# The last token group's gate stage by column halves, with the six last weight blocks run tile by tile

## The chip, the cores and the metric

The kernel runs on one core of a Trainium2 chip. A core has five engines that run side by side: TensorE (PE, matmuls), VectorE (DVE), ScalarE (ACT), GpSimd (POOL) and SyncE (SP, which here only issues DMAs). Each executes its own instructions strictly in the order in which the program lists them, and semaphores make one wait for another. The metric is device time in microseconds; the kernel before took 2855.22 us (median of three runs, 2851.17 to 2855.67).

## What is computed

One bidirectional encoder layer with shared weights runs over two sequences, a prompt of 512 tokens and a sample of 1024. The change touches the last step alone, the per-layer embedding, for the last 512 tokens of the sample:

```python
gate = jax.nn.sigmoid((group_rmsnorm(h, ple_norm_pre) @ w_ple_gate).astype(f32))
e = (p_l @ w_ple_proj).astype(f32)
h = h + group_rmsnorm((gate * e).astype(dtype), ple_norm_post)
```

`group_rmsnorm` divides a row of 1024 numbers by the root of its mean square and multiplies by a weight row. So for each token: gate times e, the sum of its squares over all 1024 columns, a scale from that sum, times the weight row, plus the residual h, and out.

## The kernel before

Tokens are worked in groups of 512, four tiles of 128 tokens each (`ORDER` is 0, 2, 1, 3). The sample has two groups, S 0 and S 1; S 1 is the last work of the program.

`ple` (L1374) makes the gate with `tok_gemm` (L1007), a matrix product of the group's 512 tokens with `w_ple_gate` (1024 by 1024). It does the 1024 output columns in two halves `nch` of 512. Within a half it goes over the 1024 input rows in blocks of 128, loaded in pairs (`k0` = 0, 2, 4, 6). Since products in fp32 are made of a rounded and a low part, a block is loaded (SP, L277, into `wst`), rounded on ACT (L292, `whi`), and its low part is made on POOL (L293, `wlo`). Each block and tile then takes three matmuls of 512 columns (`mm3`, L301 to L303). `whi` and `wlo` have six buffers each, so six blocks fit. Normally all four tiles take a pair of blocks before the next pair. In the second half of the last products (`last`) two pairs are held back and run tile by tile, so that tiles end one after another:

```python
                if last and nch == 1 and k0 + 4 >= nk:
                    if k0 + 2 < nk:
                        continue
                for t in ORDER:
                    for u0, ws in units:
```

After a half, `ev_gate` (L1383) applies the sigmoid on ACT (L1386, `mst`) and multiplies the tile's half of e by it on VectorE (L1387; the tile `ga`, which lives in the buffers named `bh`).

`ple_post` (L1392) calls `post_steps` (L1040), written for whole rows of 1024: residual load `load` (L1050, SP), `sumsq` (L312, an ACT square with accumulator, which is a second ACT instruction), `rstd` (L305: a 128x1 scalar operation on VectorE, L308, and a power on POOL, L309), then `add`. For S 1 (`last`), `add` makes the product with the weight row (L1056) ahead of the scale, then scale and residual in one instruction (L1057), and stores 128x1024 from SP (L1061). `post` runs at high priority.

The order of instructions on each engine is not the order of the code: the framework schedules them by a simulated timeline and by priorities.

Of the kernel before, what the change touches and what calls it, by code (L numbers as in the profile page):

```python
# [15 lines left out]
ALU = mybir.AluOpType  # L16
PSUM = bass.MemoryType.PSUM

D = 1024
# [3 lines left out]
NF = FFN // 128  # L23
# [143 lines left out]
class Kern:  # L167
# [143 lines left out]

    def sumsq(self, pool, x):  # L312

        ss = self.T(self.sp, [128, 1], "ss")
        junk = self.T(pool, [128, x.shape[-1]], "junk", BF16, bufs=1)
        self.nc.scalar.activation(junk, x, AF.Square, accum_out=ss)
        return ss
# [689 lines left out]
    def tok_gemm(self, lhs, nk, wsrc, krow0, evac, last=False, mid=None):  # L1007

        for nch in range(2):
# [7 lines left out]
            for k0 in range(0, nk, 2):  # L1017
# [3 lines left out]
                if mid and nch == 0 and k0 == 4:  # L1021
                    mid()
                if last and nch == 1 and k0 + 4 >= nk:
                    if k0 + 2 < nk:
                        continue
# [13 lines left out]

    def post_steps(self, pool, acc, row, res, t0, dst, gain=None, u=None, tags=("t4",) * 4, last=False):  # L1040


        nc = self.nc
# [4 lines left out]
        def load(t):  # L1048
            rts[t] = self.T(pool, [128, 1024], tags[t])
            nc.sync.dma_start(rts[t], res[t0 + t * 128:t0 + (t + 1) * 128, :])  # L1050

        def add(t):
            a, r, rt = acc[t], rs[t], rts[t]
            if last:
                w = self.T(pool, [128, 1024], "t4")
                nc.vector.tensor_tensor(out=w, in0=a, in1=rw, op=ALU.mult)  # L1056
                nc.vector.scalar_tensor_tensor(rt, w, r, rt, ALU.mult, ALU.add)  # L1057
            else:
                nc.vector.scalar_tensor_tensor(a, a, r, rw, ALU.mult, ALU.mult)
                nc.vector.tensor_tensor(out=rt, in0=a, in1=rt, op=ALU.add)  # L1060
            (nc.sync if last else nc.gpsimd).dma_start(dst[t0 + t * 128:t0 + (t + 1) * 128, :], rt)  # L1061
            if gain:
                rs[t] = self.rstd(self.sumsq(pool, rt), D)
# [36 lines left out]
    def outproj(self, q, g, pool, acc, k0, mix, u=None):  # L1100
# [10 lines left out]
        last = k0 + nk == 16  # L1111
        self.tok_gemm(mix.tok, nk, self.I["w_out"][0], k0 * 128, evac, last)
        if last:
# [8 lines left out]
    def down(self, pool, acc, hidden, m0, cnt):  # L1122

        nc = self.nc

        def evac(nch, t, ps):
            a = acc[t][:, nch * 512:(nch + 1) * 512]
            if m0 == 0:
                nc.scalar.activation(a, ps, AF.Copy)
            else:  # L1130
                nc.vector.tensor_tensor(out=a, in0=a, in1=ps, op=ALU.add)

        self.tok_gemm(lambda k, t: [x[:, t * 128:(t + 1) * 128] for x in hidden[m0 + k]], cnt,
                      self.I["w_down"][0], m0 * 128, evac, m0 + cnt == NF)

# [238 lines left out]
    def ple(self, q, g, pool, u):  # L1374
# [3 lines left out]
        def load():  # L1378
            for t in ORDER:
                r0 = g * 512 + t * 128  # L1380
                nc.sync.dma_start(ga[t], q.e[r0:r0 + 128, :])

        def ev_gate(nch, t, ps):  # L1383
            a = ga[t][:, nch * 512:(nch + 1) * 512]
            sg = self.T(pool, [128, 512], "mst")
            nc.scalar.activation(sg, ps, AF.Sigmoid)  # L1386
            nc.vector.tensor_tensor(out=a, in0=a, in1=sg, op=ALU.mult)  # L1387

        self.tok_gemm(u.tok, 8, I["w_ple_gate"][0], 0, ev_gate, True, load)
        return ga  # L1390

    def ple_post(self, q, g, pool, ga):  # L1392
        last = q is self.S and g == 1
        self.post(pool, ga, "ple_norm_post", q.h2, g * 512, q.out, last=last,
                  tags=("bh", "bl", "bl", "bh") if last else ("t4",) * 4)

    def build(self):
# [43 lines left out]
        with self.pool("mix_s", side="right") as mp, ExitStack() as right:  # L1441
# [24 lines left out]
            with self.pool("blocks") as tb:  # L1466
# [21 lines left out]
                with self.pool("end_s", side="right") as tr:  # L1488
# [5 lines left out]
                    self.rush(chain)  # L1494
                    for g, v in ((0, v0), (1, v1)):
                        self.ple_post(S, g, pe, self.ple(S, g, pe, v))

# [29 lines left out]
```

## Time and profile before

| | us |
|---|---|
| median of three runs | 2855.22 |
| lowest and highest run | 2851.17, 2855.67 |
| the profiled execution | 2852.23 |
| its span, first to last instruction | 2850.3 |
| PE busy in the span | 2683.8 (94%) |
| DVE busy | 1742.6 (61%) |
| POOL busy | 1380.7 (48%) |
| ACT busy | 1336.4 (47%) |
| mean granted TensorE clock | 0.98 |

Times in the profile are microseconds from the start of the span. A timeline row gives start, length, engine, line, operation and tiles (written <- read), the number of instructions merged into it, and in brackets how long the engine was idle before it and what ended that. A group row gives the count, busy time, mean in nanoseconds, and idle time. PEld is the weight load of a matmul, which overlaps the one before. A window row gives the busy time and the number of instructions of each engine in a stretch, then the granted clock, the busy share of the 16 DMA engines, and their GB/s. "SPq" and "ACTq" are instructions of an engine's queue that are not counted as busy, such as the issue of a DMA.

### The profile page before, as it was taken

What the parts mean: (1) busy time and instruction counts of PE and PEld (TensorE: products, weight loads), DVE (VectorE), ACT (ScalarE), POOL (GpSimd) and SP (SyncE); (2) the same over time, 40 slices, a digit from 0 to 9 for tenths busy, and PEclk for the clock granted to TensorE, in tenths of its full rate; (3) what the DMA queues carried; (4) which work ended last, traced back from release to release, by engine and by line L of the source; (5) the groups of instructions that cost most, each with busy time, mean ns of one, the idle gap of its engine ahead of it and who ended that gap; (6) DMA issues with size and microseconds to landing.
All of it is one profiled execution on the core that took longest, in us unless ns stands there. A gap on an engine that the chain in (4) does not pass through costs nothing.

```text
span 2850.3 us, 41685 instructions
## 1 busy us (share of the span) xinstructions
PE 2683.8 (94%) x14696; PEld 2254.9 (79%) x14696; DVE 1742.6 (61%) x2893; ACT 1336.4 (47%) x2580; POOL 1380.7 (48%) x1137
## 2 busy tenths in 40 slices
PE   7999999999999989889999998987799999999998
PEld 5987888778888767578778776766699999877776
DVE  6767896977666896966676734475343444325345
ACT  4434445773234564745444454365533333344453
POOL 4445555443453556535444444554454444445464
PEclk9999999999999999989999999999999999999999
DMA  5544555744345576778888886565632222366665
GB/s 169 180 137 127 150 174 185 219 141 138 99 123 160 154 249 202 223 206 206 199 181 204 187 218 218 177 222 183 157 100 82 79 75 86 119 207 207 203 202 186
DMA packets 448507, 480.04 MB, mean 168 GB/s; under 512 B 29409, under 2 KB 330281, under 8 KB 445995
## 3 DMA queue, kind: packets, MB, share of 16 engines
q1 hardware_dynamic: 340923, 347.34, 40.0%
q0 software_dynamic: 28224, 68.17, 10.8%
q10 hardware_dynamic: 79152, 61.88, 6.9%
q8 instruction: 116, 1.90, 0.3%
q14 instruction: 92, 0.75, 0.1%
HBM read 346.54 MB, written 91.95 MB: 154 GB/s over the span
## 4 chain that ended last, share of the span: by engine, by line
PE 66%; DVE 15%; DMA 8%; issue 5%; POOL 3%; ACT 2%; SPq 0%; POOLq 0%; ACTq 0%; DVEq 0%
PE g L301 17%; PE g L303 16%; PE g L302 16%; PE a L302 3%; PE a L303 3%; PE a L301 3%; PE a L700 1%; DVE b L692 1%; DVE W L619 1%; DVE E L615 1%; PE a L973 1%; POOL wlo L293 1%; DMA wlo<-wst 1%; PE a L404 1%; DMA mx<-mix_s 1%
## 5 line engine op out<-in xcount | busy, mean ns | idle before, releaser
L293 POOL TENSOR_TENSOR wlo<-wst,whi 128x512 fp32r<-128x512 f32 (+1 forms) x544 | 786.1, 1452 | 756.6 <-ACT whi L292 691.5
L292 ACT ACTIVATE whi<-wst 128x512 fp32r<-128x512 f32 (+1 forms) x544 | 339.5, 628 | 532.9 <-PE g L302 330.0
L301 PE MATMUL g<-uh,whi 128*128 128x512 f32 (+1 forms) x1232 | 493.5, 401 | 8.5 <-DVE cv L393 4.4
L303 PE MATMUL g<-uh,wlo 128*128 128x512 f32 (+1 forms) x1232 | 491.6, 399 | 0.0
L302 PE MATMUL g<-ul,whi 128*128 128x512 f32 (+1 forms) x1232 | 490.9, 398 | 0.0
L301 PE MATMUL g<-bh,whi 128*128 128x256 f32 x1056 | 293.0, 283 | 14.3 <-ACT sc L1266 3.8
L303 PE MATMUL g<-bh,wlo 128*128 128x256 f32 x1056 | 294.0, 281 | 4.2 <-DMA wlo<-mx 2.7
L302 PE MATMUL g<-bl,whi 128*128 128x256 f32 x1056 | 294.3, 280 | 0.0
L301 PEld LDWEIGHTS g<-uh,whi 128*128 128x128 f32 x1232 | 233.2, 189 | 67.5 <-issue 10.4
L303 PEld LDWEIGHTS g<-uh,wlo 128*128 128x128 f32 x1232 | 232.6, 189 | 53.9 <-issue 5.8
L302 PEld LDWEIGHTS g<-ul,whi 128*128 128x128 f32 x1232 | 232.9, 189 | 53.4 <-issue 7.2
L326 DVE TENSOR_TENSOR ml<-mx,mh 128x512 fp32r<-128x512 f32 x152 | 122.4, 808 | 222.0 <-ACT mh L325 221.9
L285 POOL DMA_DIRECT2D wlo<-wst x144 | 126.0, 930 | 226.2 <-ACT wlo L284 211.1
L393 DVE SCALAR_TENSOR_TENSOR cv<-g,cols,cv 128x510 f32<-128x510 f32 (+3 forms) x192 | 193.0, 1006 | 64.9 <-ACT cv L387 62.8
L301 PEld LDWEIGHTS g<-bh,whi 128*128 128x128 f32 x1056 | 197.2, 189 | 20.0 <-DVE gt L1227 6.1
L303 PEld LDWEIGHTS g<-bh,wlo 128*128 128x128 f32 x1056 | 199.6, 189 | 4.9 <-DMA wlo<-mx 2.9
L302 PEld LDWEIGHTS g<-bl,whi 128*128 128x128 f32 x1056 | 199.5, 189 | 0.1
L301 PE MATMUL g<-whi,mh 128*128 128x512 f32 x412 | 169.7, 412 | 23.7 <-ACT mh L325 16.3
L302 PE MATMUL g<-wlo,uh 128*128 128x264 f32 (+1 forms) x576 | 191.3, 332 | 0.5 <-POOL wlo L293 0.5
L303 PE MATMUL g<-whi,ul 128*128 128x264 f32 (+1 forms) x576 | 189.9, 331 | 1.6 <-DVE rs_t L308 1.6
L309 POOL TENSOR_TENSOR rs_t<-rs_t,nhalf 128x1 f32<-128x1 f32 (+2 forms) x112 | 120.0, 1074 | 144.0 <-DVE rs_t L308 141.5
L301 PE MATMUL g<-whi,uh 128*128 128x264 f32 (+1 forms) x576 | 189.0, 330 | 0.0
(334 smaller groups left out, 6030.5 us busy)
## 6 DMA issues: line engine op xcount, KB each, us to landing
wst<-in_w_in SPq DMA_DIRECT2D x192, 256.0 KB
wlo<-wst POOLq DMA_DIRECT2D x144, 256.0 KB, 4.9
wst<-in_w_down SPq DMA_DIRECT2D x132, 256.0 KB
wst<-in_w_out SPq DMA_DIRECT2D x96, 256.0 KB
wst<-in_w_gate SPq DMA_DIRECT2D x92, 256.0 KB
wst<-in_w_up SPq DMA_DIRECT2D x92, 256.0 KB
mx<-hid_s SPq DMA_DIRECT2D x88, 256.0 KB
rw<-rows_s SPq DMA_DIRECT2D x32, 512.0 KB
```

What stands on the lines that cost most here:

```text
L285: nc.gpsimd.dma_start(lo, w, accum_op=ALU.add)
L292: nc.scalar.activation(hi, w, AF.Copy)
L293: (eng or nc.gpsimd).tensor_tensor(out=lo, in0=w, in1=hi.bitcast(F32), op=ALU.subtract)
L301: nc.tensor.matmul(ps, lh, rh, start=first, stop=False, skip_group_check=shared)
L302: nc.tensor.matmul(ps, lh, rl, start=False, stop=False, skip_group_check=shared)
L303: nc.tensor.matmul(ps, ll, rh, start=False, stop=last, skip_group_check=shared)
L309: nc.gpsimd.tensor_tensor(out=t[:, :w], in0=t[:, :w], in1=self.nhalf[:, :w], op=ALU.pow)
L326: self.nc.vector.tensor_tensor(out=lo, in0=ps, in1=hi.bitcast(F32), op=ALU.subtract)
L393: nc.vector.scalar_tensor_tensor(out[:, a:b], ps[:, a + d:b + d], wcol(w), out[:, a:b], ALU.mult, ALU.add)
L404: nc.tensor.transpose(ps[:, j * 128:(j + 1) * 128], srcs[i + j], self.ident)
L615: nc.vector.scalar_tensor_tensor(E[:, h], rw[:, 0, h], dbf[:, c, gh:gh + 1], rw[:, 1, h], ALU.add, ALU.min)
L619: nc.vector.scalar_tensor_tensor(W[:, h], su, dt[:, c, gh:gh + 1], W[:, h], ALU.mult, ALU.add)
```

## The change

For S 1 (`end`), `ple` now does everything, and `ple_post` isn't called:

- the square is done for each half of the columns, into `hs`, and the two sums are added on VectorE when the second half is there (L1396 of the changed kernel);
- the product with the weight row is done for each half, in place (L1390);
- the residual is loaded inside the first half's evaluation (L1393), into two `t4` buffers (tiles 0 and 1) and two `bl` buffers (tiles 2 and 3), before two `bh` and two `bl`;
- scale and residual are done as two halves (L1400), each stored by itself (L1401), the first from SP and the second from ACT;
- in the second column half three pairs of blocks are held back in place of two (`last` = 3), so blocks 2 to 7 run tile by tile;
- nothing of it runs at high priority any more.

`last` of other products becomes 2, which leaves them as they were; `post_steps` loses its `last` branch.

```diff
-                if last and nch == 1 and k0 + 4 >= nk:
+                if last and nch == 1 and k0 + last * 2 >= nk:
...
+        end = q is self.S and g == 1
+        hs = self.T(self.sp, [128, 2, 4], "hss", bufs=1) if end else None
+        res = {}
+
         def ev_gate(nch, t, ps):
             a = ga[t][:, nch * 512:(nch + 1) * 512]
             sg = self.T(pool, [128, 512], "mst")
             nc.scalar.activation(sg, ps, AF.Sigmoid)
             nc.vector.tensor_tensor(out=a, in0=a, in1=sg, op=ALU.mult)
-
-        self.tok_gemm(u.tok, 8, I["w_ple_gate"][0], 0, ev_gate, True, load)
+            if not end:
+                return
+            self.sumsq(pool, a, hs[:, nch, t:t + 1])
+            nc.vector.tensor_tensor(out=a, in0=a, in1=rw[:, nch * 512:(nch + 1) * 512], op=ALU.mult)
+            if nch == 0:
+                res[t] = self.T(pool, [128, 1024], "t4" if t < 2 else "bl")
+                nc.sync.dma_start(res[t], q.h2[g * 512 + t * 128:g * 512 + (t + 1) * 128, :])
+                return
+            ss = hs[:, 0, t:t + 1]
+            nc.vector.tensor_tensor(out=ss, in0=ss, in1=hs[:, 1, t:t + 1], op=ALU.add)
+            r = self.rstd(ss, D)
+            for i, eng in enumerate((nc.sync, nc.scalar)):
+                cs = slice(i * 512, (i + 1) * 512)
+                nc.vector.scalar_tensor_tensor(res[t][:, cs], ga[t][:, cs], r, res[t][:, cs], ALU.mult, ALU.add)
+                eng.dma_start(q.out[g * 512 + t * 128:g * 512 + (t + 1) * 128, cs], res[t][:, cs])
+
+        if end:
+            rw = self.gain_row(pool, "row", "ple_norm_post")
+        self.tok_gemm(u.tok, 8, I["w_ple_gate"][0], 0, ev_gate, 3 if end else 2, load)
...
-                    for g, v in ((0, v0), (1, v1)):
-                        self.ple_post(S, g, pe, self.ple(S, g, pe, v))
+                    self.ple_post(S, 0, pe, self.ple(S, 0, pe, v0))
+                    self.ple(S, 1, pe, v1)
```

What this makes of the order on three engines is shown at three places. First PE, in the second column half of S 1, from the 7th matmul behind blocks 0 and 1. Before, where `a_27149` and `a_27151` are the accumulators of tiles 0 and 2, and `whi_27191` and `whi_27197` blocks 2 and 3:

```order
L301 MATMUL a_27151<-whi_27191,bh_26472 128x512
L302 MATMUL a_27151<-wlo_27192,bh_26472 128x512
L303 MATMUL a_27151<-whi_27191,bl_26476 128x512
L301 MATMUL a_27151<-whi_27197,bh_26472 128x512
L302 MATMUL a_27151<-wlo_27198,bh_26472 128x512
```

In the changed kernel, where `a_27172` and `a_27174` are tiles 0 and 2, and `whi_27214`, `27220`, `27226`, `27232` blocks 2 to 5 (27238 and 27244, further on, are blocks 6 and 7):

```order
L301 MATMUL a_27172<-whi_27226,bh_26473 128x512
L302 MATMUL a_27172<-wlo_27227,bh_26473 128x512
L303 MATMUL a_27172<-whi_27226,bl_26477 128x512
L301 MATMUL a_27172<-whi_27232,bh_26473 128x512
L301 MATMUL a_27174<-whi_27214,bh_26472 128x512
L302 MATMUL a_27174<-wlo_27215,bh_26472 128x512
L302 MATMUL a_27172<-wlo_27233,bh_26473 128x512
L303 MATMUL a_27172<-whi_27232,bl_26477 128x512
L303 MATMUL a_27174<-whi_27214,bl_26476 128x512
```

Tile 0 goes on with blocks 4 and 5 where tile 2 had blocks 2 and 3, and the scheduler has put tile 2's matmuls between tile 0's; the two share the first 36 of the 72 matmuls, and tiles 1 and 3 follow with 18 each. The low part of block 6 is used first by the 27th of the 72, that of block 7 by the 32nd.

Second ACT, at the end of the first column half of S 1 (g_26987 and g_26990 hold tiles 0 and 2, g_26988 and g_26991 tiles 1 and 3; the four `whi` are blocks 4 to 7 of the second half). Before:

```order
L1386 ACTIVATE mst_27137<-g_26987 128x512
L1386 ACTIVATE mst_27140<-g_26987 128x512
L292 ACTIVATE whi_27227<-wst_27225 128x512
L1386 ACTIVATE mst_27143<-g_26988 128x512
L1386 ACTIVATE mst_27146<-g_26988 128x512
L292 ACTIVATE whi_27233<-wst_27231 128x512
L292 ACTIVATE whi_27239<-wst_27237 128x512
L292 ACTIVATE whi_27245<-wst_27243 128x512
```

In the changed kernel:

```order
L1385 ACTIVATE mst_27140<-g_26990 128x512
L1385 ACTIVATE mst_27148<-g_26990 128x512
L316 ACTIVATE junk_27143,hss_26987<-bh_26983 128x512
L292 ACTIVATE whi_27226<-wst_27224 128x512
L316 ACTIVATE junk_27151,hss_26987<-bh_26985 128x512
L1385 ACTIVATE mst_27156<-g_26991 128x512
L1385 ACTIVATE mst_27164<-g_26991 128x512
L292 ACTIVATE whi_27232<-wst_27230 128x512
L316 ACTIVATE junk_27159,hss_26987<-bh_26984 128x512
L316 ACTIVATE junk_27167,hss_26987<-bh_26986 128x512
L292 ACTIVATE whi_27238<-wst_27236 128x512
L292 ACTIVATE whi_27244<-wst_27242 128x512
```

Four squares stand among the roundings of the last four blocks.

Third VectorE, at the end of the program (bh_26984 is tile 1, bh_26986 tile 3 in both). Before:

```order
L1387 TENSOR_TENSOR bh_26986<-bh_26986,mst_27306 128x512
L1057 SCALAR_TENSOR_TENSOR bl_27347<-t_5322_27349,rs_t_27330,bl_27347 128x1024
L1056 TENSOR_TENSOR t_5324_27355<-bh_26986,row_27309 128x1024
L308 TENSOR_SCALAR rs_t_27336<-ss_27333 128x1
L1057 SCALAR_TENSOR_TENSOR bh_27353<-t_5324_27355,rs_t_27336,bh_27353 128x1024
```

In the changed kernel (t_5278_27162 and bl_27170 are the residuals of tiles 1 and 3; the rows marked x2 are two halves):

```order
L1386 TENSOR_TENSOR bh_26984<-bh_26984,mst_27348 128x512
L1390 TENSOR_TENSOR bh_26984<-bh_26984,row_26988 128x512
L1396 TENSOR_TENSOR hss_26987<-hss_26987 128x1
L1386 TENSOR_TENSOR bh_26986<-bh_26986,mst_27362 128x512
L308 TENSOR_SCALAR rs_t_27355<-hss_26987 128x1
L1400 SCALAR_TENSOR_TENSOR t_5278_27162<-bh_26984,rs_t_27355,t_5278_27162 128x512 x2
L1390 TENSOR_TENSOR bh_26986<-bh_26986,row_26988 128x512
L1396 TENSOR_TENSOR hss_26987<-hss_26987 128x1
L308 TENSOR_SCALAR rs_t_27369<-hss_26987 128x1
L1400 SCALAR_TENSOR_TENSOR bl_27170<-bh_26986,rs_t_27369,bl_27170 128x512 x2
```

Behind the last gate product (L1387 before, L1386 now), tile 1's two final halves still stand ahead of tile 3's row product, as tile 1's final product did before. On ACT, the two stores of tiles 0 and 2 stand ahead of tile 1's square.

On POOL nothing changes its place. On SP, the first two residual loads (now tiles 2 and 3) stand a few places later, behind the first loads of e for S 1; that of tile 0 stands between the weight loads of blocks 4 and 5 of the second half, that of tile 1 behind block 7.

More of the change, by code (lines that the diff above doesn't have):

```diff
@@ L310, in rstd, with sumsq @@
         return t[:, :w]
-    def sumsq(self, pool, x):
-        ss = self.T(self.sp, [128, 1], "ss")
+    def sumsq(self, pool, x, ss=None):
+        ss = self.T(self.sp, [128, 1], "ss") if ss is None else ss
         junk = self.T(pool, [128, x.shape[-1]], "junk", BF16, bufs=1)
@@ L1038, in post, with post_steps @@
             pass
-    def post_steps(self, pool, acc, row, res, t0, dst, gain=None, u=None, tags=("t4",) * 4, last=False):
+    def post_steps(self, pool, acc, row, res, t0, dst, gain=None, u=None):
         nc = self.nc
@@ L1048, in load @@
         def load(t):
-            rts[t] = self.T(pool, [128, 1024], tags[t])
+            rts[t] = self.T(pool, [128, 1024], "t4")
             nc.sync.dma_start(rts[t], res[t0 + t * 128:t0 + (t + 1) * 128, :])
@@ L1053, in add @@
             a, r, rt = acc[t], rs[t], rts[t]
[L1054 to L1061, printed above, removed]
+            nc.vector.scalar_tensor_tensor(a, a, r, rw, ALU.mult, ALU.mult)
+            nc.vector.tensor_tensor(out=rt, in0=a, in1=rt, op=ALU.add)
+            nc.gpsimd.dma_start(dst[t0 + t * 128:t0 + (t + 1) * 128, :], rt)
             if gain:
@@ L1111, in outproj @@
         last = k0 + nk == 16
-        self.tok_gemm(mix.tok, nk, self.I["w_out"][0], k0 * 128, evac, last)
+        self.tok_gemm(mix.tok, nk, self.I["w_out"][0], k0 * 128, evac, 2 * last)
         if last:
@@ L1133, in down @@
         self.tok_gemm(lambda k, t: [x[:, t * 128:(t + 1) * 128] for x in hidden[m0 + k]], cnt,
-                      self.I["w_down"][0], m0 * 128, evac, m0 + cnt == NF)
+                      self.I["w_down"][0], m0 * 128, evac, 2 * (m0 + cnt == NF))
     def ffn(self, q, g, pool, u):
@@ L1387, in ev_gate @@
             nc.vector.tensor_tensor(out=a, in0=a, in1=sg, op=ALU.mult)
-        self.tok_gemm(u.tok, 8, I["w_ple_gate"][0], 0, ev_gate, True, load)
+            if not end:
[16 more added lines that the diff above has]
+        self.tok_gemm(u.tok, 8, I["w_ple_gate"][0], 0, ev_gate, 3 if end else 2, load)
         return ga
     def ple_post(self, q, g, pool, ga):
-        last = q is self.S and g == 1
-        self.post(pool, ga, "ple_norm_post", q.h2, g * 512, q.out, last=last,
-                  tags=("bh", "bl", "bl", "bh") if last else ("t4",) * 4)
+        self.post(pool, ga, "ple_norm_post", q.h2, g * 512, q.out)
     def build(self):
```

## The prediction

> **What bounds the kernel now.** I read the totals first, then the busy time of every engine in short stretches of the end, then each engine's timeline of the last 35 us, and last the groups that price operations in shapes which the end does not hold yet.
>
> ```profile
> span 2850.3 us, 41685 instructions
> PE 2683.8 (94%) x14696; PEld 2254.9 (79%) x14696; DVE 1742.6 (61%) x2893; ACT 1336.4 (47%) x2580; POOL 1380.7 (48%) x1137
> ...
> core 0: us, PE busy (x) PEld busy (x) DVE busy (x) ACT busy (x) POOL busy (x), PEclk, DMA share, GB/s
> ...
> 2780.00:2782.00 2.00, 2.00 (x10) 1.60 (x9) 0.69 (x1) 0.54 (x2) 0.00 (x0) 1.00 1.03 420
> ...
> 2820.00:2830.00 10.00, 10.00 (x45) 8.11 (x44) 0.83 (x1) 1.26 (x2) 2.82 (x3) 1.00 0.01 2
> ...
> 2836.00:2838.00 2.00, 2.00 (x10) 1.60 (x10) 1.85 (x4) 0.76 (x3) 0.67 (x1) 1.00 0.55 225
> 2838.00:2840.00 2.00, 0.99 (x5) 0.47 (x3) 1.71 (x2) 1.62 (x3) 0.26 (x1) 1.00 0.09 37
> ```
>
> PE is busy in every microsecond up to 2838.99 (10.00 of 10.00, then 2.00 of 2.00), at full granted clock. Behind it stands a tail of 2850.3 - 2838.99 = 11.3 us without one matmul. The order of all engines is the same in both kernels up to the last group of the last projection, so the change can win only in that tail, and lose only there or by making PE wait. The next rows are PE's first and last of the second column half that the change reorders, and VectorE's last eight. (A row is start, length, engine, line, operation, tiles; the bracket is idle time before it.)
>
> ```profile
> 2822.17 0.40 PE L301 MATMUL a<-whi,bh 128*128 128x512 f32 x1
> ...
> 2838.59 0.40 PE L303 MATMUL g<-whi,bl 128*128 128x512 f32 x1
> ```
> ```profile
> 2838.29 1.28 DVE L1057 SCALAR_TENSOR_TENSOR bl<-t,rs_t,bl 128x1024 f32<-128x1024 f32 x1 [0.44 <-POOL rs_t L309]
> 2839.49 1.22 DVE L1056 TENSOR_TENSOR t<-bh,row 128x1024 f32<-128x1024 f32 x1
> 2840.63 0.15 DVE L308 TENSOR_SCALAR rs_t<-ss 128x1 f32<-128x1 f32 x1
> 2840.69 0.68 DVE L1387 TENSOR_TENSOR bh<-bh,mst 128x512 f32<-128x512 f32 x1
> 2841.81 1.28 DVE L1057 SCALAR_TENSOR_TENSOR bl<-t,rs_t,bl 128x1024 f32<-128x1024 f32 x1 [0.43 <-POOL rs_t L309]
> 2843.01 1.22 DVE L1056 TENSOR_TENSOR t<-bh,row 128x1024 f32<-128x1024 f32 x1
> 2844.15 0.14 DVE L308 TENSOR_SCALAR rs_t<-ss 128x1 f32<-128x1 f32 x1
> 2844.95 1.28 DVE L1057 SCALAR_TENSOR_TENSOR bh<-t,rs_t,bh 128x1024 f32<-128x1024 f32 x1 [0.66 <-POOL rs_t L309]
> ```
>
> One tile costs VectorE 2841.81 - 2838.29, about 3.5 us, while PE delivers one every twelve matmuls, 2.8 us: VectorE falls behind, and its last product ends at 2846.23, 7.24 us after the last matmul. So the tail is a VectorE queue, then one store.
>
> ```profile
> 2846.26 0.33 SPq L1061 DMA_DIRECT2D out<-bh  x1
> ```
> ```profile
> 2846.60:2846.90 0.30, 0.00 (x0) 0.00 (x0) 0.00 (x0) 0.00 (x0) 0.00 (x0) 0.50 0.00 0
> 2846.90:2847.20 0.30, 0.00 (x0) 0.00 (x0) 0.00 (x0) 0.00 (x0) 0.00 (x0) 0.50 0.44 177
> ...
> 2848.10:2848.40 0.30, 0.00 (x0) 0.00 (x0) 0.00 (x0) 0.00 (x0) 0.00 (x0) 0.50 0.84 341
> 2848.40:2848.70 0.30, 0.00 (x0) 0.00 (x0) 0.00 (x0) 0.00 (x0) 0.00 (x0) 0.50 0.02 0
> ```
>
> From the DMA share: the store is issued at 2846.26, moves from about 2847.07 (0.44 of that slice) to about 2848.36, so 0.8 us to start and 1.29 us for 512 KB. Another 1.94 us pass to the end of the span.
>
> **The matmuls.** None is added. From 2822.17 there are 72, one per (2838.59 - 2822.17)/71 = 0.2313 us. The order lists show that tiles 0 and 2 are not done one by one but interleaved over the first 36; tile 0 ends with the 33rd, tile 2 with the 36th, tile 1 with the 54th, tile 3 with the 72nd. Starts are 2822.17 + 0.2313 n, ends 0.40 later: **2829.97, 2830.66, 2834.83 and, unchanged, 2838.99**. Before, with twelve per tile from the 25th on, they ended at 2830.67, 2833.44, 2836.22, 2838.99.
>
> **The last tiles on VectorE.** The shapes become 128x512 nearly everywhere. Prices of shapes that this place lacks come from groups elsewhere; they are a square with its accumulator read, a product with a scalar, and a DMA issued by ACT.
>
> ```profile
> L316 ACT ACTIVATE junk<-y 128x512 bf16<-128x512 f32 x24 | 15.0, 624 | 14.4 <-POOL y L647 14.4
> L316 ACT ACTIVATION_READ_ACCUMULATOR junk<-y 128x1 f32 x24 | 4.6, 192 | 0.0
> L790 DVE SCALAR_TENSOR_TENSOR b<-b 128x512 f32<-128x512 f32 x8 | 5.5, 686 | 0.0
> ...
> L1371 ACTq DMA_DIRECT2D e_s<-mx x16: 326/326/445, 1970.8 to 2015.3; - x16
> ...
> L1313 ACTq DMA_DIRECT2D hid_s<-gt x44: 326/521/585, 2067.8 to 2480.8; - x44
> ```
> ```profile
> 2839.02 0.60 ACT L1386 ACTIVATE mst<-g 128x512 f32<-128x512 f32 x1
> ...
> 2840.86 0.92 POOL L309 TENSOR_TENSOR rs_t<-rs_t,nhalf 128x1 f32<-128x1 f32 x1 [2.60 <-DVE rs_t L308]
> 2844.37 0.54 POOL L309 TENSOR_TENSOR rs_t<-rs_t,nhalf 128x1 f32<-128x1 f32 x1 [2.59 <-DVE rs_t L308]
> ```
>
> By these, tiles 0 and 2 (sigmoids from 2830.00 and 2830.70, then product, square, row product, sum, power, two final halves each) leave VectorE at about 2837.1. Tile 1's gate product follows at once, its square ends near 2838.5, its row product and sum near 2839.2. ACT's two store issues (0.33 each) stand ahead of tile 1's square, but the second waits for the same VectorE instruction that tile 1's product waits for, and is done while that product runs: nothing. All this is over before the last sigmoid ends, with 0.4 us to spare.
>
> From the last matmul the order decides, since VectorE takes its rows in sequence:
> - sigmoid 0.60 from 2839.02, gate product of tile 3 0.68: 2840.33
> - **tile 1's remainder stands ahead of tile 3's**: scalar op to 2840.42, 0.08 to POOL, power 0.54 (VectorE is idle beside it, as at 2844.37), then two halves of 0.69 that overlap by 0.07: 2842.39
> - tile 3's row product 0.69 (its square has long ended, 2841.1): 2843.00; sum of halves, priced as a 128x1 scalar op, 0.15: 2843.08; scalar op 2843.26; power 2843.88; halves 2843.92 to 2844.61 and 2844.54 to **2845.23**.
>
> That is 1.00 us before 2846.23. The sum-of-halves add in 128x1 is in no row here; I bound it by nothing and by the 0.69 of a 128x512 product, and take 0.15, the row of its size.
>
> **The two stores.** The first half is issued at 2844.64 and moves 0.8 us later, 2845.44 to 2846.09 (half of 1.29). The second is issued on ACT at 2845.26 and moves 2846.09 to 2846.74. With the same 1.94 us behind it the span ends at 2848.68: **1.62 us less**, 1.00 from VectorE and 0.62 from the shorter last transfer. How long ACT's queue needs to its first packet is in no row of the end; bounds are 0 and 0.64 us of loss (no gain from the size), and I take SP's 0.8 as the nearest row. The Trainium skill, SBUF — State Buffer, The DMA setup-cost knee (why "@ 1 MiB" ≠ asymptote), advises the largest single transfer, since each pays a nearly fixed 2 us; by its fit, an estimate, half the bytes save 0.6 us if the second transfer's fixed part runs beside the first.
>
> **Loads.** Four residual loads of 512 KB stay four. Two now stand between or behind the weight loads on SP, each waiting for a store of group 0.
>
> ```profile
> 2803.87 0.58 POOL L1061 DMA_DIRECT2D out<-t  x1
> ...
> out<-t POOLq DMA_DIRECT2D x4, 512.0 KB, 3.9
> ...
> 2805.88 7.62 SPq L277 DMA_DIRECT2D wst<-in_w_ple_gate  x4
> ```
> ```profile
> 2816.15 0.63 ACT L292 ACTIVATE whi<-wst 128x512 fp32r<-128x512 f32 x1 [1.03 <-issue]
> ...
> 2821.72 1.33 ACT L292 ACTIVATE whi<-wst 128x512 fp32r<-128x512 f32 x2 [3.15 <-issue]
> ...
> 2814.66 6.17 DVE L1387 TENSOR_TENSOR bh<-bh,mst 128x512 f32<-128x512 f32 x4 [3.91 <-ACT mst L1386]
> ...
> 2816.86 3.42 POOL L293 TENSOR_TENSOR wlo<-wst,whi 128x512 fp32r<-128x512 f32 x2 [0.61 <-ACT whi L292]
> 2822.43 2.54 POOL L293 TENSOR_TENSOR wlo<-wst,whi 128x512 fp32r<-128x512 f32 x2 [2.15 <-ACT whi L292]
> ...
> L1387 DVE TENSOR_TENSOR bh<-bh,mst x8: 678/692/2144, 2814.7 to 2840.7; 128x512 f32<-128x512 f32 x8
> ```
>
> The first of them, ahead of the last three weight loads, waits for the store of 2803.87, landed near 2808.4 by the 3.9 of the queue; the second stands behind all weights. The last weights were issued by 2805.88 + 7.62 = 2813.5 and rounded on ACT at 2821.72, so a load that comes 1 to 2 us later costs nothing.
>
> **Rivals.**
>
> *PE waits for weights.* ACT now does four squares (0.72 each with the read) between the roundings of the last four weight blocks; each waits for a gate product on VectorE, and four row products are queued among these. Beside POOL's splits such a product took up to 2.144 us, against a median of 0.692. With 2.14 for the first, as now, it goes: product to 2816.8, square to 2817.5, rounding to 2818.1; second product 2817.5, square 2818.8, two sigmoids and a rounding to 2820.5; four more products at 0.7 to 1.6 to 2823.0; the last square to 2823.7, the last two roundings to 2825.0. POOL's splits at 1.3 to 1.9 each (2.54 and 3.42 for two) end at 2825.7 and 2827.0, or 2826.3 and 2828.2. PE's interleaved order asks for these two as its 27th and 32nd matmul, at 2828.2 and 2829.3: covered by 1.1 us or more. With 2.14 for all eight products the roundings end near 2828.7 and 2829.3, the splits near 2830 and 2832.2, and PE stalls 2.9 us. Net that is 2.9 - 1.6, **1.3 us slower than before**: profiled 2853.5. It decides as soon as the last split ends after 2829.3. For it speaks the 2.144; against it the median. The Trainium skill, SBUF — State Buffer, Who interferes with whom, says that a VectorE instruction with two SBUF inputs and a GpSimd instruction that reads SBUF hold a shared port by exclusive lock, the loser blocked for the whole instruction. By that rule every added row product may stretch a split or be stretched; the 2.144, and the power's 0.92 beside 0.54, agree, and the stall would be the one just worked out.
>
> *The halves pay in series.* If the second store starts only when the first has landed, it moves from 2844.64 + 0.8 + 0.65 + 1.94 = 2848.0 to 2848.7, and the span ends at 2850.6, 0.3 us slower. Against it: many loads in one queue keep the DMA engines at a share of 1.03 (2780 to 2782), with no pause for a landing. The page just named for stores would give this if the fixed part came twice.
>
> *The last tile finishes alone*, as the diff reads. Without tile 1's remainder ahead, tile 3's square, which ends at 2841.1, comes last, and 1.8 us more go: 3.4 us less, profiled 2848.8. The order of VectorE speaks against it.
>
> *It does nothing.* Powers of 0.92 twice (+0.76), no gain from half the bytes (+0.64) and a slow ACT issue (+0.25) eat the 1.62.
>
> **How the numbers follow.** The profiled execution took 2852.23, 1.93 more than its span; it would take 2850.6. It lies 3.0 below the median of the runs, 2855.22 (2851.17 to 2855.67); executions differ by more than the change is worth. I take the middle of these four executions, (2852.23 + 2855.22)/2 = 2853.7, less 1.6: **2852.1**. The forecast holds with 0.75; late weights 0.12, doing nothing or stores in series 0.09, a tile that finishes alone 0.04. Gains of 0 to 2.3 us (the latter if halves cost half of the 1024 rows and small ops nothing) give 2851.17 - 2.3 = 2848.9 as low end; 2855.67 and the 0.3 of the second rival give 2856.0. A difference under 0.2%, 5.7 us, can hardly be told from no change here, and no case reaches it by its mechanism: within 0.2% has 0.85. What remains is the spread of the executions, which with a small gain falls more often on the fast side: faster 0.11, slower 0.04.
>
> **What would show it.** Right: PE busy without a gap to 11.3 us less 1.6 before the end; tiles' sigmoids near 2830.0, 2830.7, 2834.9, 2839.0; the last VectorE product 6.2 us after the last matmul, with two halves of tile 1 between the last gate product and its row product; the last packets 1.5 us after the last issue. Wrong: a PE gap between 2826 and 2831; powers of 0.9 in the last 5 us; a pause between the two stores' packets.

## The result, and the profile after

| | before | changed |
|---|---|---|
| median, us | 2854.36 | 2863.02 |
| lowest and highest, us | 2851.17, 2860.51 | 2855.1, 2870.48 |
| runs | 11 | 11 |
| profiled execution, us | 2852.23 | 2855.1 |
| its span, us | 2850.3 | 2853.1 |

The ratio is 1.0030, with a 95% interval of 1.0018 to 1.0042: the changed kernel is 8.7 us **slower**, and its median lies above the range. The profiled execution of the changed kernel is its fastest, so the two profiles differ by less than the medians.

The totals on the changed kernel's page; then, from its timeline, PE's last row, VectorE's last rows, the last two powers on POOL, and the last store issues of SP and ACT:

```profile
span 2853.1 us, 41716 instructions
PE 2694.8 (94%) x14696; PEld 2263.7 (79%) x14696; DVE 1752.6 (61%) x2905; ACT 1338.1 (47%) x2588; POOL 1373.6 (48%) x1137
```
```profile
2842.31 0.39 PE L303 MATMUL g<-whi,bl 128*128 128x512 f32 x1
```
```profile
2843.37 0.69 DVE L1386 TENSOR_TENSOR bh<-bh,mst 128x512 f32<-128x512 f32 x1 [0.45 <-ACT mst L1385]
2843.97 0.15 DVE L308 TENSOR_SCALAR rs_t<-hss 128x1 f32<-128x1 f32 x1
2844.77 1.42 DVE L1400 SCALAR_TENSOR_TENSOR t<-bh,rs_t,t 128x512 f32<-128x512 f32 x2 [0.65 <-POOL rs_t L309]
2846.11 0.69 DVE L1390 TENSOR_TENSOR bh<-bh,row 128x512 f32<-128x512 f32 x1
2846.71 0.15 DVE L1396 TENSOR_TENSOR hss<-hss 128x1 f32<-128x1 f32 x1
2846.89 0.15 DVE L308 TENSOR_SCALAR rs_t<-hss 128x1 f32<-128x1 f32 x1
2847.70 1.42 DVE L1400 SCALAR_TENSOR_TENSOR bl<-bh,rs_t,bl 128x512 f32<-128x512 f32 x2 [0.66 <-POOL rs_t L309]
```
```profile
2844.20 0.54 POOL L309 TENSOR_TENSOR rs_t<-rs_t,nhalf 128x1 f32<-128x1 f32 x1 [5.69 <-DVE rs_t L308]
2847.13 0.54 POOL L309 TENSOR_TENSOR rs_t<-rs_t,nhalf 128x1 f32<-128x1 f32 x1 [2.39 <-DVE rs_t L308]
```
```profile
2848.49 0.33 SPq L1401 DMA_DIRECT2D out<-bl  x1
...
2849.15 0.34 ACTq L1401 DMA_DIRECT2D out<-bl  x1
```

The tail did get shorter: VectorE ends at 2849.12, 6.42 us after the last matmul (2842.70), where it was 7.24; the span ends 10.4 us after it, where it was 11.3. But the last matmul itself comes at 2842.70 instead of 2838.99, and PE is busy for 11.0 us longer with the same 14,696 matmuls (not all of that is loss: experiment 1 below, which loses nothing, has 2690.3 against 2683.8). The time is lost ahead of the tail, where both kernels list the same instructions in the same order.

Where? The windows below are 200 us of the gate and up products, a steady stretch: PE 99% busy at full granted clock. Columns: stretch, its length, PE busy and the number of matmuls, granted clock, DMA share, GB/s; then the first and last start of the stage's first matmul of three (`bh` streams through the weights `whi`). Before:

```profile
2220.00:2320.00 100.00, 99.27 (x842) 1.00 0.27 80
2320.00:2420.00 100.00, 99.51 (x844) 1.00 0.27 80
```
```profile
L301 PE MATMUL g<-bh,whi x1056: 276/280/415, 2011.5 to 2477.7; 128*128 128x256 f32 x176
```

Changed:

```profile
2220.00:2320.00 100.00, 99.26 (x830) 1.00 0.26 76
2320.00:2420.00 100.00, 99.50 (x833) 1.00 0.27 80
```
```profile
L301 PE MATMUL g<-bh,whi x1056: 276/280/582, 2011.7 to 2483.5; 128*128 128x256 f32 x176
```

PE is as busy, at the same clock, but finishes 1,663 matmuls in 200 us in place of 1,686: 120.3 ns each instead of 118.6. The stage begins at the same time and ends 5.8 us later. It has 3,696 matmuls of this kind (three lines, each with 1,056 that write `g` and 176 that write `a`); 3,696 times 1.64 ns is 6.1 us.

What differs between the kernels there is not the instructions but where the tiles lie. The changed kernel allocates one more small tile, `hs`, 32 bytes in each partition, in a pool that lies ahead of `uh` and `bh` and lives for the whole program. 464 tiles behind it move up by 32 bytes, all others stay. Some start addresses in the two built programs, with their remainder by 64:

```
         before         changed
ident    16512   0      16512   0
whi      30848   0      30848   0
uh       57216   0      57248  32
bh       57216   0      57248  32
bl      114560   0     114592  32
hh       98176   0      98208  32
mh      217056  32     217056  32
```

**Theory A:** a matmul takes about 2 ns longer where an operand that TensorE reads starts 32 bytes off a multiple of 64. **Rival B:** the tail, or the longer program, costs the time by itself. **Rival C:** chance of that session.

### The profile page after: what moved, and what is told of

Same layout as the page of the kernel before. It is cut to its first block, busy times and chain, and to the rows that moved or that the text cites. A ratio compares the mean times of both kernels' runs of the same rounds, so it can differ in the third digit from the quotient of the medians.

```text
span 2853.1 us, 41716 instructions
## 1 busy us (share of the span) xinstructions
PE 2694.8 (94%) x14696; PEld 2263.7 (79%) x14696; DVE 1752.6 (61%) x2905; ACT 1338.1 (47%) x2588; POOL 1373.6 (48%) x1137
## 4 chain that ended last, share of the span: by engine, by line
PE 70%; DVE 14%; DMA 7%; issue 5%; POOL 3%; ACT 2%; SPq 0%; DVEq 0%; POOLq 0%; ACTq 0%
PE g L301 18%; PE g L303 17%; PE g L302 17%; PE a L303 3%; PE a L302 3%; PE a L301 3%; PE a L700 2%; PE a L973 1%; DVE E L615 1%; DMA mx<-mix_s 1%; POOL wlo L293 1%; DVE b L692 1%; DVE W L619 1%; PE a L404 1%; PE a L628 1%
## 5 line engine op out<-in xcount | busy, mean ns | idle before, releaser
L302 PE MATMUL g<-ul,whi 128*128 128x512 f32 (+1 forms) x1232 | 490.8, 398 | 0.0
L302 PE MATMUL g<-bl,whi 128*128 128x256 f32 x1056 | 297.0, 283 | 0.0
L302 PEld LDWEIGHTS g<-ul,whi 128*128 128x128 f32 x1232 | 232.7, 189 | 53.8 <-issue 6.9
L302 PEld LDWEIGHTS g<-bl,whi 128*128 128x128 f32 x1056 | 200.4, 190 | 0.1
L302 PE MATMUL g<-wlo,uh 128*128 128x264 f32 (+1 forms) x576 | 192.0, 334 | 0.0
```

The source lines that it names most:

```text
L302: nc.tensor.matmul(ps, lh, rl, start=False, stop=False, skip_group_check=shared)
```

## Experiments

Twelve kernels ran, each beside the kernel before on the same chip; none leaves out work. The measured numbers of all are in a table at the end of this section.

**1 to 4. The displacement alone, and the change without it.**

```diff
-        hs = self.T(self.sp, [128, 2, 4], "hss", bufs=1) if end else None
+        hs = self.cols[:, :, 120:124] if end else None
```

> The whole change, but its small tile of eight sums is a slice of a constant tile that is no longer used, so that every other tile lies at the address it has in the kernel before; in the changed kernel 464 tiles lie 32 bytes higher. Theory A (the 32 bytes slow the whole program, the tail itself gains): 0.9 to 1.6 us below before, ratio 0.9994 to 0.9997. Rival B (the tail itself, or the length of the program's code, costs the time): as the changed kernel, 8 to 9 us above before, ratio 1.003. Rival C (chance of that session): within 2 us of before, as all others of this set.

The kernel before with an unused tile of 32 bytes:

```diff
+        if last:
+            self.T(self.sp, [128, 2, 4], "hss", bufs=1)
```

> The kernel before with an unused tile of 32 bytes in the same pool: the same instructions, 464 tiles 32 bytes higher. Theory A: 9 to 10.5 us above before (the loss of the changed kernel without the gain of its tail), ratio 1.0031 to 1.0037. Rival B: as before, ratio 1.000. Rival C: as before.

The change with a tile twice as wide:

```diff
-        hs = self.T(self.sp, [128, 2, 4], "hss", bufs=1) if end else None
+        hs = self.T(self.sp, [128, 2, 8], "hss", bufs=1) if end else None
```

> The whole change with the small tile twice as wide, so that the 464 tiles lie 64 bytes higher, at multiples of 64 again. Theory A in the form that counts the alignment: 0.9 to 1.6 us below before, as the first kernel of this set. Theory A in the form that counts any displacement: 8 to 9 us above before. Rival B: 8 to 9 us above before too. Rival C: within 2 us of before.

The kernel before with an unused tile of 64 bytes (`[128, 2, 8]` in the second diff):

> The kernel before with an unused tile of 64 bytes in the same pool. Theory A by alignment: as before, ratio 1.000. Theory A by any displacement: 9 to 10 us above before. Rivals B and C: as before. With the third kernel this tells the displacement from the program's tail.

Measured ratios: the change without displacement 1.0004 (0.9993 to 1.0015); the kernel before with 32 bytes **1.0027 (1.0016 to 1.0038)**; the change with 64 bytes 1.0005 (0.9993 to 1.0016); the kernel before with 64 bytes 1.0008 (0.9996 to 1.0020). An unused tile costs the kernel before about as much as the whole change cost it (a little under the 1.0031 that A expected at least), and no loss is seen in the change without the displacement. That rules out B and C. A displacement by 64 does no such harm: the ratios alone overlap, but the same 200 us hold 1,689 matmuls with 64 bytes and 1,660 with 32. So it is the remainder that counts. The expected gain of 0.9 to 1.6 us is not seen in any median: it is a third to a half of an interval's half-width. The windows of the kernel before with 32 bytes:

```profile
2220.00:2320.00 100.00, 99.27 (x828) 1.00 0.26 75
2320.00:2420.00 100.00, 99.51 (x832) 1.00 0.28 81
```
```profile
L301 PE MATMUL g<-bh,whi x1056: 276/280/419, 2012.7 to 2484.7; 128*128 128x256 f32 x176
```

This is the changed kernel's picture, without the change: the stage takes 472.0 us (471.8 in the changed kernel, 466.2 before).

**5. Only the operands of that stage put right again, in the changed kernel.** All else stays 32 bytes off.

```diff
             with self.pool("blocks") as tb:
+                self.T(tb, [128, 8], "pad1", bufs=1)
```

> The changed kernel, its small tile and the displacement of 32 bytes kept, with 32 more bytes ahead of bh and bl alone, so that these lie at multiples of 64 again. Theory A (3,696 matmuls that stream bh or bl carry most of the loss): 842 to 844 matmuls in 100 us, and 6 to 7 of the 8 us come back: ratio 1.000 to 1.001. Rival F (the loss is spread over all displaced tiles, their DMAs and VectorE's work among them): ratio 1.002 to 1.003 as the changed kernel.

Measured: 1.0008 (0.9998 to 1.0017). The windows are back:

```profile
2220.00:2320.00 100.00, 99.27 (x844) 1.00 0.26 77
2320.00:2420.00 100.00, 99.51 (x846) 1.00 0.28 83
```

So most of the loss is in the matmuls that read `bh` and `bl`. What the other displaced tiles cost, through other matmuls, DMAs, ACT or VectorE, cannot be told from nothing: the interval reaches from 0.6 us below before to 4.8 us above, with the shorter tail in it.

**6. One of the two operands off, in the kernel before.**

```diff
-        self.parts = [[kern.T(pool, [128, 4, 256], t, F32R) for _ in range(7)] for t in ("bh", "bl")]
+        self.parts = []
+        for t in ("bh", "bl"):
+            self.parts.append([kern.T(pool, [128, 4, 256], t, F32R) for _ in range(7)])
+            kern.T(kern.tb, [128, 8], "pad2", bufs=1)
...
+                self.tb = tb
+                self.T(tb, [128, 8], "pad1", bufs=1)
```

> The kernel before with 32 unused bytes ahead of the tiles bh and 32 behind them, so that of all left tiles bh alone lies 32 bytes off a multiple of 64, and bl at one. Theory A: in the 470 us of the gate and up products the matmuls of L301 and L303, which stream bh, take about 2 ns more each, those of L302, which stream bl, as before; some 834 matmuls in 100 us at full clock, between 843 and 829; the first to the last of them 4 to 5 us longer than the 466 of before. Rival F (the loss is in what writes or evicts, or in the memory as a whole): all three lines move alike, or none.

```profile
2220.00:2320.00 100.00, 99.22 (x833) 1.00 0.26 78
2320.00:2420.00 100.00, 99.48 (x836) 1.00 0.27 80
```
```profile
L304 PE MATMUL g<-bh,whi x1056: 276/281/415, 2009.8 to 2479.0; 128*128 128x256 f32 x176
```

(In this kernel the three lines are L304 to L306.) 1,669 matmuls lie between 1,686 and 1,663, 17 of the 23 that both operands cost; the stage took 469.2 us, 3.0 more than before where 4 to 5 were expected. The split by line is not as expected: the distance from a matmul's start to the next, worked out from the starts in the trace, rose at all three lines. (Each figure is the mean of a group's sorted distances between one tenth and seven tenths of them. Over the middle half the figures, here and below, are up to 1.5 ns higher, and `bh` and `bl` rise by 1.1 to 1.5 ns in the changed kernel in place of 1.5 to 2.2.)

```
ns from start to next start     before  changed  5: bh,bl put right  6: bh alone off
L301 bh streams, whi loaded      116.1    117.6         115.6             118.1
L302 bl streams, whi loaded      116.0    118.2         115.4             117.4
L303 bh streams, wlo loaded      115.7    117.5         115.4             116.9
```

That `bl`'s line rises too is what rival F said of lines that move alike; that about two thirds of the loss comes with the one tile is what A said. Matmuls overlap here (280 ns long, 116 ns apart), so a distance need not belong to the matmul at whose start it begins; this attribution stays open, the sum does not.

**7 and 8. A forecast from theory A: tiles that are off in the kernel before.** `mh` and `ml`, loaded as weights by 1,920 matmuls, lie 32 bytes off in both kernels.

```diff
-        with self.pool("mix_s", side="right") as mp, ExitStack() as right:
+        with self.pool("pad", side="right") as pad, self.pool("mix_s", side="right") as mp, ExitStack() as right:
+            self.T(pad, [128, 8], "pad")
```

> The kernel before with 32 unused bytes at the right end of the memory for the last part of the program, so that the tiles mh, ml, mx, acc, row, t4, sc and gt, which lie 32 bytes off a multiple of 64 in the kernel before, lie at multiples of 64. Theory A (a matmul costs about 2 ns more where an operand that TensorE reads starts off a multiple of 64): the 1,920 matmuls with mh or ml follow each other at 230 to 231.5 ns in place of 232.1 to 232.5, up to 2.9 us in all, of which 1 to 3 us show in the end. Rival D (only the operand that streams counts, and mh and ml are the weights that are loaded): these distances and the time stay within 1 us.

```
ns from start to next start     before   7: mix_s moved   8: right end moved
L301 whi streams, mh loaded      232.1       230.7            230.6
L302 wlo streams, mh loaded      232.3       229.9            229.7
L303 whi streams, ml loaded      232.5       230.2            230.2
```

The matmuls did speed up by 1.4 to 2.4 ns, so rival D falls: the loaded operand counts as well as the streaming one. But the time went to **1.0016** (1.0004 to 1.0028), against the expectation. The rows show one place: PE's last start with `uh` and first with `mh`, of the kernel before and of this one.

```profile
L301 PE MATMUL g<-uh,whi x1232: 276/393/799, 23.8 to 1672.2; 128*128 128x512 f32 x172, 128*128 128x256 f32 x4
...
L301 PE MATMUL g<-whi,mh x412: 388/396/794, 1697.8 to 2744.2; 128*128 128x512 f32 x138
```
```profile
L301 PE MATMUL g<-uh,whi x1232: 276/393/799, 23.6 to 1679.4; 128*128 128x512 f32 x172, 128*128 128x256 f32 x4
...
L301 PE MATMUL g<-whi,mh x412: 387/394/796, 1709.5 to 2756.6; 128*128 128x512 f32 x138
```

25.6 us between them became 30.1. (That `uh` itself ends 7 us later is not the pad's, which comes after it; this was the slowest execution of the twelve.) In experiment 9, which has the same pad, the stretch is 31.1 us; in the twelve profiles without it, it is 24.5 to 27.9. The pad moved this pool but not the tiles of the convolution that lay there earlier, so the new tiles overlap others of those, and may have to wait for them. With the pad from the program's start all right tiles move alike:

```diff
+        self.T(self.ctx.enter_context(self.pool("pad", side="right")), [128, 8], "pad")
         self.stream("m")
```

> The kernel before with the 32 unused bytes at the right end from the program's start, so that all right tiles move alike and each lies over the same earlier tiles as before. Theory J (the 4 to 5 us that the later pad lost between the last matmul with uh and the first with mh came from new overlaps with tiles of the convolution): that stretch is 24 to 27 us again (25.1 before, 29.6 with the later pad), mh and ml's matmuls follow each other at 230 to 231 ns, and the time is 0 to 3 us below before, ratio 0.9990 to 1.0000. Rival K (tiles at multiples of 64 on the right cost by themselves): ratio 1.001 or more, as with the later pad.

```profile
L302 PE MATMUL g<-uh,whi x1232: 276/394/799, 23.8 to 1671.0; 128*128 128x512 f32 x172, 128*128 128x256 f32 x4
...
L302 PE MATMUL g<-whi,mh x412: 387/393/777, 1695.7 to 2738.0; 128*128 128x512 f32 x138
```

The three lines are L302 to L304 here. 24.7 us, the same faster matmuls, and 0.9992 (0.9981 to 1.0004). That is as J expects and speaks against K; that this kernel is faster than the one before is likely but not shown, since the interval holds 1. Which tiles overlapped is not shown.

**9 and 10. What bounds the tail.** First tile 1 finished whole ahead of tile 3, by a column of ones that is computed from tile 1's result (with the pad of experiment 7, and `hs` as in experiment 1).

```diff
...
+            if nch == 1 and t == ORDER[-1]:
+                one = hs[:, 0, ORDER[0]:ORDER[0] + 1]
+                nc.vector.tensor_scalar(one, res[ORDER[-2]][:, 1023:1024], 0.0, 1.0, ALU.mult, ALU.add)
+                nc.vector.scalar_tensor_tensor(a, a, one, sg, ALU.mult, ALU.mult)
+            else:
+                nc.vector.tensor_tensor(out=a, in0=a, in1=sg, op=ALU.mult)
```

> The whole change without the displacement, with the right end aligned as in the kernel ahead, and with tile 1's last products put ahead of tile 3's gate product on VectorE (through a column of ones that is computed from tile 1's result). Theory A and the tail as measured: from the end of the last matmul to the end of the span 10.4 less 1.8, 8.6 us (11.3 before); with the matmuls of mh and ml 3 to 5 us below before in all, ratio 0.998 to 0.999. Rival D: 2.7 us below before, all of it behind the last matmul. Rival E (VectorE's order is not what bounds the tail): 10.4 us stay.

It came out worse: 11.4 us from the last matmul to the end, and 1.0011 (1.0000 to 1.0021). The last matmul ends at 2843.69. ACT's row is tile 3's sigmoid; VectorE's are tile 1's two halves, then tile 3's gate product, row product and two halves:

```profile
2843.73 0.60 ACT L1385 ACTIVATE mst<-g 128x512 f32<-128x512 f32 x1 [0.54 <-PE g L303]
...
2844.82 1.42 DVE L1406 SCALAR_TENSOR_TENSOR t<-bh,rs_t,t 128x512 f32<-128x512 f32 x2 [0.65 <-POOL rs_t L309]
...
2846.53 0.75 DVE L1392 SCALAR_TENSOR_TENSOR bh<-bh,cols,mst 128x512 f32<-128x512 f32 x1
2848.07 0.69 DVE L1396 TENSOR_TENSOR bh<-bh,row 128x512 f32<-128x512 f32 x1 [0.79 <-ACT junk L316]
...
2849.67 1.41 DVE L1406 SCALAR_TENSOR_TENSOR bl<-bh,rs_t,bl 128x512 f32<-128x512 f32 x2 [0.66 <-POOL rs_t L309]
```

Tile 3's sigmoid has ended at 2844.33, but its gate product stands behind tile 1's halves and starts only at 2846.53. Then the row product, which overwrites the half that ACT's square still reads, waits 0.79 us, and the power makes VectorE wait 0.66 more. In the changed kernel the gate product comes first, and tile 1's work fills the wait for the square. So the row product gets a tile of its own, and tile 1's final halves stand between tile 3's sum and its scale:

```diff
-            nc.vector.tensor_tensor(out=a, in0=a, in1=rw[:, nch * 512:(nch + 1) * 512], op=ALU.mult)
+            w = self.T(pool, [128, 512], "mh") if nch else a
+            nc.vector.tensor_tensor(out=w, in0=a, in1=rw[:, nch * 512:(nch + 1) * 512], op=ALU.mult)
...
+                to = (ga[ORDER[-1]] if i else rw)[:, 512:1024] if t == ORDER[-2] else res[t][:, cs]
+                nc.vector.scalar_tensor_tensor(to, w if i else ga[t][:, cs], rs[t], res[t][:, cs], ALU.mult, ALU.add)
+                eng.dma_start(q.out[g * 512 + t * 128:g * 512 + (t + 1) * 128, cs], to)
+
+            if t == ORDER[-1]:
+                late.pop(0)()
             ss = hs[:, 0, t:t + 1]
             nc.vector.tensor_tensor(out=ss, in0=ss, in1=hs[:, 1, t:t + 1], op=ALU.add)
...
+            rs[t] = self.rstd(ss, D)
+            if t == ORDER[-1]:
+                late.pop(0)()
+            jobs = [functools.partial(half, i, eng) for i, eng in enumerate((nc.sync, nc.scalar))]
+            if t == ORDER[-2]:
+                late.extend(jobs)
+                return
...
```

> The whole change without the displacement, and in its tail the row product of a second column half goes to a tile of its own (so that it need not wait for the square that reads the same half), and on VectorE tile 3's row product and sum stand ahead of tile 1's two last halves, whose results go to the gain row and to tile 3's gate half, both read for the last time by then. Theory H (VectorE's order bounds the tail; the wait for tile 1's power is covered now): from the end of the last matmul to the end of the span 9.6 to 9.9 us, against 10.4 of the change and 11.3 before. Rival I (something else bounds it, as when tile 1 was put ahead whole and 11.3 came): 10.4 or more. In the total 1.5 us below before, less than can be told.

```profile
2840.38 0.40 PE L303 MATMUL g<-whi,bl 128*128 128x512 f32 x1
```
```profile
2841.44 0.69 DVE L1386 TENSOR_TENSOR bh<-bh,mst 128x512 f32<-128x512 f32 x1 [1.02 <-ACT mst L1385]
2842.16 0.69 DVE L1391 TENSOR_TENSOR mh<-bh,row 128x512 f32<-128x512 f32 x1
...
2844.36 0.14 DVE L308 TENSOR_SCALAR rs_t<-cols 128x1 f32<-128x1 f32 x1
2845.16 0.75 DVE L1399 SCALAR_TENSOR_TENSOR bl<-bh,rs_t,bl 128x512 f32<-128x512 f32 x1 [0.66 <-POOL rs_t L309]
2845.83 0.74 DVE L1399 SCALAR_TENSOR_TENSOR bl<-mh,rs_t,bl 128x512 f32<-128x512 f32 x1
```

The last product ends 5.8 us after the last matmul, and the span (2850.5) 9.7 us after it, as expected by H: what VectorE does in which order does bound the tail. The tile of its own and the new order were not tried apart. In the total, 1.0002 (0.9991 to 1.0013), such a gain of 1.6 us cannot be told.

**11. Both.** Experiments 8 and 10 in one kernel.

> The tail of the first kernel of this set with the right end of the second. Theories H and J: 1.5 to 4.5 us below before, ratio 0.9984 to 0.9995. Rival K: 1.000 to 1.001.

The tail is the same 9.7 us, the total 1.0002 (0.9989 to 1.0014). That is where K puts it and not the gain that H and J add up to, but the interval also holds a part of that gain; that the two add up is not shown. No version here is shown to beat the kernel before. The lowest ratio is that of the pad alone, experiment 8.

**12. The last store.** The change as in experiment 1, with both halves on SP:

```diff
-            for i, eng in enumerate((nc.sync, nc.scalar)):
+            for i, eng in enumerate((nc.sync, nc.sync)):
```

> The whole change without the displacement, both stores of a tile issued by SP. From the end of VectorE's last product to the end of the span the kernel before needs 4.07 us and the change 3.98. Theory L (the store on ACT's queue starts later or is reported later than one on SP's): 3.4 to 3.7. Rival M (the fixed part of a store's time does not depend on the queue, and grows where two are under way): 3.9 to 4.1.

```profile
span 2845.5 us, 41716 instructions
```
```profile
2840.08 1.41 DVE L1400 SCALAR_TENSOR_TENSOR bl<-bh,rs_t,bl 128x512 f32<-128x512 f32 x2 [0.66 <-POOL rs_t L309]
```

2845.5 less 2841.49 is 4.0 us, as M expects: it is not ACT's queue. Why the time behind the last packet grew is not shown by this.

| kernel | median, us | runs | ratio to before (95%) | matmuls in the 200 us | tail, us |
|---|---|---|---|---|---|
| changed kernel | 2863.02 | 11 | 1.0030 (1.0018 to 1.0042) | 1,663 | 10.4 |
| 1 change, no displacement | 2851.84 | 12 | 1.0004 (0.9993 to 1.0015) | 1,686 | 10.4 |
| 2 before, 32 bytes | 2858.53 | 12 | 1.0027 (1.0016 to 1.0038) | 1,660 | 11.3 |
| 3 change, 64 bytes | 2852.50 | 12 | 1.0005 (0.9993 to 1.0016) | 1,688 | 10.4 |
| 4 before, 64 bytes | 2853.39 | 12 | 1.0008 (0.9996 to 1.0020) | 1,689 | 11.3 |
| 5 change, bh and bl put right | 2854.48 | 11 | 1.0008 (0.9998 to 1.0017) | 1,690 | 10.4 |
| 6 before, bh alone off | 2853.81 | 1 | | 1,669 | 11.4 |
| 7 before, last part moved | 2855.60 | 12 | 1.0016 (1.0004 to 1.0028) | 1,684 | 11.3 |
| 8 before, right end moved | 2849.60 | 12 | 0.9992 (0.9981 to 1.0004) | 1,684 | 11.3 |
| 9 tile 1 first, with 7 | 2855.89 | 11 | 1.0011 (1.0000 to 1.0021) | 1,686 | 11.4 |
| 10 tail in another order | 2851.55 | 12 | 1.0002 (0.9991 to 1.0013) | 1,685 | 9.7 |
| 11 both | 2853.63 | 12 | 1.0002 (0.9989 to 1.0014) | 1,686 | 9.7 |
| 12 both stores on SP | 2847.47 | 1 | | 1,685 | 10.4 |

The kernel before had medians of 2850.99 (35 runs, experiments 1 to 4), 2851.97 (29, experiments 5, 6, 7 and 9) and 2851.51 (29, the rest). The tail is the time from the end of the last matmul to the end of the span, in the profiled execution.

## Why the prediction was wrong

**The step that failed** is the second sentence behind the first view: "The order of all engines is the same in both kernels up to the last group of the last projection, so the change can win only in that tail, and lose only there or by making PE wait." The first half is true. The conclusion took the same order for the same time. The same instructions in the same order ran slower, since their tiles lay 32 bytes further on: 1.64 ns on each of 3,696 matmuls, 6.1 us. Since the tail gave back about 1 us, 9.7 us have to be explained at the medians; the interval of the net loss reaches from 5.1 to 12 us. The matmuls that stream `uh` may hold part of the rest: the first of their three lines rose from 231.2 to 233.3 ns, and 1,200 of these at 2.1 ns are 2.5 us, an estimate. The stage with them lasted 1,645.0 to 1,655.8 us in the fourteen profiles, which varies too much to show it. The sum of the prediction has no term for the diff's line that allocates `hs` for the whole program, and gives no reason for leaving it out. The profile of before holds only a faint trace of the effect: worked out as above, matmuls that load `mh`, which is off, follow each other at 232.1 to 232.5 ns, those that load `bh` or `bl` at 229.6 to 230.8. But the addresses could be had from the built program, and a comparison of them would have asked the question. Why an operand at such an address costs TensorE time is open.

The Trainium skill, SBUF — State Buffer, Operand start alignment, says of an operand's start that it must be a multiple of its element size, which is about legality, and that its runs timed nothing. All starts here obey that. The runs add a price at 32 bytes past a multiple of 64.

**The tail** went as worked out, with a smaller sum. Measured from the end of the last matmul:

- The last sigmoid's start and tile 3's gate product (forecast end +1.34, measured +1.36), tile 1's halves ahead of tile 3's row product (end +3.40, measured +3.49), and the last two powers, 0.54 each, held. VectorE's last product ended at +6.42 for a forecast +6.24: a gain of 0.82 us, not 1.00, since each of the two pairs of halves took 1.42 in place of 1.31.
- The sum of halves, bounded by nothing and 0.69, took the 0.15 that was chosen.
- **The stores were mis-sized.** From VectorE's last product to the end of the span it was 4.1 us before and 3.9 to 4.0 in the change; 0.62 was forecast and 0.1 came. The rival of halves in series didn't happen either: the packets ran on without a pause, as the DMA share of the changed kernel shows. In the first line each digit is the share, in tenths, of one of 40 slices from 2846.0 to 2853.1 (the first run of digits is tile 1's store, the second tile 3's); in the others it is the second last column.

```profile
DMA  0079999999100000002999999952000000000000
```
```profile
2849.30:2849.50 0.20, 0.50 0.89 338
...
2850.50:2850.70 0.20, 0.50 0.93 358
2850.70:2850.90 0.20, 0.50 0.34 82
2850.90:2851.10 0.20, 0.50 0.00 0
```

  They move from 2849.3 to 2850.8, 1.5 us for the 512 KB that took 1.29 as one store, and then 2.3 us pass to the end where 1.94 passed before. With both on SP the sum is the same. The forecast carried the fixed part of 1.94 over unchanged and split 1.29 in two; both grew. The Trainium skill, SBUF — State Buffer, The DMA setup-cost knee, which the prediction set beside its sum, advises the largest single transfer; that the split brought 0.1 us is in line with the advice, and not with the 0.6 us estimated from its fit.

- **PE did not wait for weights**, the first rival: 17.00 of 17.00 us busy from the first of the 72 matmuls to the last.

```profile
2825.70:2842.70 17.00, 17.00 (x73) 1.00 0.17 62
```

- "The last tile finishes alone" was priced at 3.4 us of gain. Experiment 9 put tile 1's remainder ahead of all of tile 3 and lost 1.0 against the change instead. The forecast of this rival said nothing of where tile 1's remainder would go (there it held tile 3's gate product back by 2.2 us), and it left out that the row product overwrites what the square reads (0.79 us of waiting), so that a tile alone is a chain of waits. Experiment 10, where other work fills the waits, gained 0.6 over the change.

So the mechanism of the tail was right, 0.96 us for a forecast 1.62, and it was covered by an effect some ten times as large, which the prediction excluded with one word, "only". The chance of slower, 0.04, followed from that word.

## What to carry to other kernels

When a change allocates anything, compare the start addresses of all tiles before and after, above all of those that the matmuls read, for a long-lived pool moves everything behind it. Where an unrelated stage gets slower with the same instructions, count instructions in equal windows at full clock: busy shares say nothing there, since a busy engine stays busy. An unused tile of the same size in the old kernel tells at once whether it is the code or its place; and a pad that cures one stage can cost time in another, as in experiment 7; moving the whole side of the memory, as in experiment 8, avoided that here.

## What the runs showed that was not expected

- With `bh` and `bl`, streamed, 32 bytes off a multiple of 64, a matmul is followed by the next after 117.5 to 118.2 ns in place of 115.4 to 116.1 (256 columns); with `mh` and `ml`, loaded, 32 bytes off, after 232.1 to 232.5 in place of 229.7 to 230.7 (512 columns). No tile that these matmuls read starts at a remainder other than 0 or 32.
- With 512 columns of `uh` streaming, only the first of the three matmuls showed it (231.2 to 233.3 ns; the others rose by 0.1 to 0.6). With `uh` loaded, the rise was 1.5 ns where 512 columns streamed and none where 264 did (120.9 and 120.7 ns). So the price is not one figure for every matmul, and why is open.
- Half the bytes in the last store saved 0.1 us of 4.1, on one queue or two.
